# A two-layer hybrid decoder step: which products share the attention rounds, and where the gates are computed

## The chip, the cores and the metric

The kernel runs on one core of one Trainium2 chip. The metric is the device time of one launch in microseconds (us). A core has TensorE for matmuls (PE; its weight loads are PEld), VectorE (DVE), ScalarE (ACT), GpSimd (POOL) and SyncE (SP, which here only issues DMAs). Line numbers L... are those of the kernel before.

## The reference

Two groups of tokens go through two layers: a prompt of 256 positions and 8 samples of 8 positions each (together T = 320 columns), model width 1024. Each layer computes

```
xn = RMSNorm(x);  h = xn @ w_in                       # 1024 x 7344, split into the parts below
A: causal means over 2/4/8/16 positions minus the token, a 128 x 128 map per group, * silu(z_pool)
B: latent attention with 8 heads; the samples attend to 2048 cached positions each, * silu(z_mla)
C: a convolution over 4 positions on q, k, v; L2 norms; a chunked gated delta rule, 8 heads; * silu(z_dn)
gates = sigmoid(h_gate)                               # 3 branches x 1024
merged = gates[0] * (y_a @ w_br_pool) + gates[1] * (y_b @ w_br_mla) + gates[2] * (y_c @ w_br_dn)
x = x + merged @ w_out
```

After the second layer comes a last RMSNorm. Keys, conv rows, pooling rows and delta states are outputs too.

## The kernel before, in words

Activations stand transposed, features on the 128 partitions and the 320 tokens along the free dimension. A product in near-float32 precision is made of three: weights and activations are each split into a high and a low part in fp32r, and `mm3` (L214 to L226) issues high x high, high x low and low x high for each of the 8 (or 4) blocks of 128 rows. So 128 columns of `w_in` or `w_out` take 24 matmuls of 128 x 128 weights and 320 columns, and 128 columns of a branch matrix (512 rows) take 12. `load_w` (L178) fetches the raw weights through SP into one of four buffers; `split_w` (L186) writes the high part on ACT (L200) and the low part on DVE (L201), or on POOL where the running number of the split in the layer stands in the table entry 'lo'.

Each layer runs through these stages:

1. *Convolution.* `unit` (L535) projects 128 columns of q or k, scales them by `rn` on DVE (L500, L501), applies four taps (the first on ACT, three on DVE at L509), tanh on ACT, and a square on POOL (L542) for the L2 norm. POOL also copies the last rows for the state output (L503, L504). `value` does the same for v, `pooling` and `pool_gate` handle branch A, `zproj` (L434) the z of the other branches. These are *fillers*, taken from a list in the order of the table entry 'fo' by `fill(n)` (L705).
2. *Inversion.* The delta rule needs the inverse of a triangular matrix for each chunk; it is built by DVE steps (L760 to L774) and three levels of small products (L789 to L820), with fillers between them (entries 'f8', 'fy', 'fz').
3. *U and W, then delta.* The chunk products, and a loop over five chunks that carries the state, again with fillers ('ft', 'fu', 'fn'): late z's, queries and keys.
4. *Heads.* Attention of the prompt, head by head, with two gates between them.
5. *Rounds.* Eight rounds bb, one for each sample: scores against its 2048 gathered keys (144 matmuls, L1186), a maximum and an exponential, the turning of the weights by transposes (L1234), the product with the values (L1257), while DVE turns the next sample's keys (L1176).
6. *End.* Branch products for 8 blocks m and three branches n, sums in `accs`, then `w_out` and the norm of the next layer.

A gate (`gate_w`, `gate_mm`, `gate_out`, L451 to L468) is 24 matmuls, a product with `rn` on DVE (L464) and a tanh on ACT (L465). The 24 gates of a layer are independent of all else after xn, so they are put wherever PE might idle, in the order of the list `order`: all three branches for blocks 0 and 1, then 2 and 3, and so on. The table entries 'ga', 'gm', 'gb', 'gc', 'gs', 'gq' say how many go behind the decay products, behind each inversion level, and so on; `GL` says how many go into each round. A gate stays in one of 11 SBUF buffers (tag gt) or is *spilled*: written to DRAM through ACT's queue and read back through POOL's (L1353) when its branch product is due. `branch_out` (L1350) multiplies product and gate on DVE; branch 0 writes the sum `accs[m]`, the other two are added to it on POOL (L1361).

In the heads, the rounds and the start of the end stage the order on each engine is the program's (`manual_schedule`, L1369). Elsewhere a planner orders the instructions of each engine from estimated times; a DMA goes out in its queue's order. Each engine then works strictly in its order.

## Time and profile before

| | |
|---|---|
| median of 3 runs | 1044.32 us (1042.73 to 1047.79) |
| the profiled execution | 1044.8 us, of which 1042.8 us are the span from the first to the last instruction |
| PE, PEld, DVE, ACT, POOL busy | 987.6, 865.2, 712.1, 466.5, 332.2 us |
| mean granted clock of TensorE | 0.973 |
| HBM read, written | 144.17 MB, 13.68 MB |

Busy times overlap, since the engines work side by side. A granted clock of 1.00 is the higher of the two levels (2.4 GHz), 0.5 the lower (1.2 GHz); a mean between them tells how much of a stretch ran at either.

In layer 0 the convolution runs from about 26 to 103 us, the inversion to 169, U, W, delta and heads to 314, the rounds to 449, the end stage to 528. Layer 1 repeats this: convolution 528 to 613, inversion to 667, rounds from 816, end from 950.

### The profile page before, as it was taken

To read this page: it belongs to the slowest core of one execution; us is meant where nothing else is said; L and a number is where in the kernel's file an instruction comes from. 1 tells how busy PE (TensorE), PEld (TensorE's weight loads), DVE (VectorE), ACT (ScalarE), POOL (GpSimd) and SP (SyncE) were. 2 spreads that over 40 slices of the span, in tenths; PEclk is the share of its full clock that TensorE was granted. 3 is DMA by queue.
4 is the path that set the end of the run, shared out by engine and by line. 5 is a ranking of instruction groups with operands and counts; after the bars stand their busy time and mean duration, and the time that the engine had idled before them with its cause. 6 is when DMAs were issued, how large, how long until landed. Compare 5 with 4: busy or idle time off the path is not lost.

```text
span 1042.8 us, 24809 instructions
## 1 busy us (share of the span) xinstructions
PE 987.6 (95%) x10211; PEld 865.2 (83%) x10211; DVE 712.1 (68%) x1353; ACT 466.5 (45%) x838; POOL 332.2 (32%) x467
## 2 busy tenths in 40 slices
PE   8988899999999999999989979999999999998996
PEld 6877798997878888789978868999887787877996
DVE  3899974658656666677758988646774675754962
ACT  5554253555443333444546534336455333334453
POOL 3656312124250101035445542221334201100631
PEclk8999899999999999999999989999999999999999
DMA  9533324633656776268563333455256577633861
GB/s 235 158 82 101 96 74 111 184 96 91 203 171 202 242 233 225 78 196 233 144 194 94 86 98 82 109 144 140 71 145 232 163 227 259 189 135 126 237 171 51
DMA packets 202698, 159.22 MB, mean 153 GB/s; under 512 B 27704, under 2 KB 191826, under 8 KB 200010
## 3 DMA queue, kind: packets, MB, share of 16 engines
q1 hardware_dynamic: 176364, 98.47, 34.7%
q0 software_dynamic: 7424, 48.75, 13.2%
q10 hardware_dynamic: 18798, 10.44, 3.5%
q8 instruction: 80, 1.31, 0.5%
q14 instruction: 32, 0.26, 0.1%
HBM read 144.17 MB, written 13.68 MB: 151 GB/s over the span
## 4 chain that ended last, share of the span: by engine, by line
PE 73%; DVE 16%; ACT 5%; issue 3%; DMA 2%; POOL 1%; SPq 0%; DVEq 0%; ACTq 0%; POOLq 0%
PE sc L1186 6%; PE pv L1257 6%; PE pj L224 5%; PE gate L224 5%; PE pj L226 5%; PE pj L225 5%; PE gate L226 5%; PE gate L225 4%; DVE cy L509 4%; DVE wl L201 3%; PE br L226 3%; PE br L224 3%; PE br L225 3%; PE wo L224 2%; PE wo L225 2%
## 5 line engine op out<-in xcount | busy, mean ns | idle before, releaser
L201 DVE TENSOR_TENSOR wl<-wraw,wh 128x1024 fp32r<-128x1024 f32 (+2 forms) x169 | 195.9, 1167 | 83.0 <-ACT wh L200 82.0
L200 ACT ACTIVATE wh<-wraw 128x1024 fp32r<-128x1024 f32 (+1 forms) x180 | 166.5, 935 | 156.4 <-PE pj L225 75.8
L224 PE MATMUL pj<-xnH,wh 128*128 128x320 f32 (+1 forms) x528 | 172.7, 327 | 13.0 <-DVE V L501 7.6
L226 PE MATMUL pj<-xnH,wl 128*128 128x320 f32 (+1 forms) x528 | 170.2, 322 | 6.3 <-DVE wl L201 6.0
L225 PE MATMUL pj<-xnL,wh 128*128 128x320 f32 (+1 forms) x528 | 168.6, 319 | 0.0
L224 PE MATMUL gate<-xnH,wh 128*128 128x320 f32 x384 | 125.4, 326 | 1.7 <-DVE V L501 1.5
L226 PE MATMUL gate<-xnH,wl 128*128 128x320 f32 x384 | 121.2, 316 | 2.2 <-DVE wl L201 1.8
L225 PE MATMUL gate<-xnL,wh 128*128 128x320 f32 x384 | 120.1, 313 | 0.0
L224 PEld LDWEIGHTS pj<-xnH,wh 128*128 128x128 f32 (+1 forms) x528 | 101.8, 193 | 19.0 <-ACT wh L200 7.7
L226 PEld LDWEIGHTS pj<-xnH,wl 128*128 128x128 f32 (+1 forms) x528 | 101.7, 193 | 10.6 <-DVE wl L201 7.9
L225 PEld LDWEIGHTS pj<-xnL,wh 128*128 128x128 f32 (+1 forms) x528 | 101.7, 193 | 4.9 <-issue 3.5
L224 PEld LDWEIGHTS gate<-xnH,wh 128*128 128x128 f32 x384 | 73.4, 191 | 9.3 <-issue 5.7
L1176 DVE STREAM_TRANSPOSE KT<-kv 128x1024 f32<-128x1024 f32 x64 | 78.6, 1228 | 0.5
L226 PEld LDWEIGHTS gate<-xnH,wl 128*128 128x128 f32 x384 | 73.3, 191 | 4.0 <-DVE wl L201 2.6
L225 PEld LDWEIGHTS gate<-xnL,wh 128*128 128x128 f32 x384 | 73.5, 191 | 1.1 <-issue 0.8
L224 PE MATMUL br<-yH,wh 128*128 128x320 f32 x192 | 61.1, 319 | 3.0 <-ACT wh L200 2.6
L226 PE MATMUL br<-yH,wl 128*128 128x320 f32 x192 | 60.4, 316 | 1.8 <-DVE wl L201 1.8
L225 PE MATMUL br<-yL,wh 128*128 128x320 f32 x192 | 60.2, 314 | 0.0
L1186 PE MATMUL sc<-KT,q 32*64 32x256 f32 x2048 | 59.3, 377 | 0.0
L1257 PE MATMUL pv<-kv,PT 128*64 128x256 f32 x512 | 58.8, 382 | 0.2
L509 DVE SCALAR_TENSOR_TENSOR cy<-V,prm,cy 128x344 f32<-128x344 f32 x72 | 56.4, 802 | 0.5
L1186 PEld LDWEIGHTS sc<-KT,q 32*64 32x64 f32 x2048 | 45.8, 131 | 12.0 <-issue 5.7
(410 smaller groups left out, 2045.1 us busy)
## 6 DMA issues: line engine op xcount, KB each, us to landing
wraw<-in_w_in SPq DMA_DIRECT2D x114, 512.0 KB
wraw<-in_w_out SPq DMA_DIRECT2D x16, 512.0 KB
q<-q4d SPq DMA_DIRECT2D x64, 72.0 KB
gate<-gt ACTq DMA_DIRECT2D x28, 160.0 KB
gt<-gate POOLq DMA_DIRECT2D x28, 160.0 KB, 3.5
wraw<-in_w_br_pool SPq DMA_DIRECT2D x16, 256.0 KB
wraw<-in_w_br_dn SPq DMA_DIRECT2D x16, 256.0 KB
wraw<-in_w_br_mla SPq DMA_DIRECT2D x16, 256.0 KB
```

What stands on the lines that cost most here:

```text
L200: act(h, raw, AF.Copy)
L201: (nc.gpsimd.tensor_tensor if spare or turn[0] in K["lo"] else tt)(lo, raw, h.bitcast(F32), sub)
L224: nc.tensor.matmul(out, wh[:, k, :], xh[:, first + k, :], start=k == 0, stop=False)
L225: nc.tensor.matmul(out, wh[:, k, :], xl[:, first + k, :], start=False, stop=False)
L226: nc.tensor.matmul(out, wl[:, k, :], xh[:, first + k, :], start=False, stop=k == nk - 1)
L509: stt(y, V[:, j : j + 344], wj(j), y, mult, add)
L1176: nc.vector.transpose(v[:, a], kv[:, a * 1024 : a * 1024 + 1024].rearrange("p (i k c) -> p i k c", i=4, k=8))
L1186: nc.tensor.matmul(sc[64 * hf : 64 * hf + 64, g, :256], q4[r, k, :], krT[r, keys_] if k == 8 else KT[r, k, keys_], start=k == 0, stop=k == 8,)
L1257: nc.tensor.matmul(pv[64 * hf : 64 * hf + 64, :256], PT[:, n * 128 + 64 * hf : n * 128 + 64 * hf + 64], kv[:, r : r + 256], start=n == 0, ...
```

## The change

- `order` holds the gates of branches 1 and 2 only, 16 of them. All are spilled to DRAM. They are all computed before the rounds: one behind the small columns and one behind the next unit ('g0'), three inside the list of fillers (entry -1 in 'fo'), one behind the decay products, one behind each of the first two inversion levels, one in the U/W part, three in the delta loop, two behind it, two in the heads.
- Each round computes the gate of branch 0 for m = bb, directly followed by that branch's product for the same m; gate times product goes to DRAM as `sums[m]` (through ACT's queue) and is read back as the start of `accs[m]` (through POOL's). The split of `zs[0..3]` that these products need moves from the last round to the end of the delta stage.
- The end stage has 16 branch products, those of branches 1 and 2, instead of 23, and in layer 1 no late gate any more.
- Squares (L542) and the state copies (two on POOL, now a strided one) move to ACT. 'lo' is empty: every low part of a weight split is made on DVE.

Table entries that differ (before, then after; where the layers differ, layer 0 / layer 1):

| entry | what it counts | before | after |
|---|---|---|---|
| kk | fillers around the decay products | 1, 1, 2, 3 | 2, 1, 3, 4 |
| g0 | gates behind the small columns, behind the next unit | none | 1, 1 |
| ga | gates behind the decay products | 3 | 1 |
| fy | fillers between a level's two products | 2, 1, 1 / 2, 1, 2 | 2, 2, 2 |
| fz | fillers behind a level | 1, 1, 1 / 1, 0, 1 | 1, 1, 2 |
| gm | gates behind a level | 0, 2, 0 / 0, 0, 0 | 1, 1, 0 |
| gb | gates behind the inversion | 0 / 1 | 0 |
| gc | gates in the U/W part | 0, 0, 0 | 0, 1, 0 |
| gs | gates in the delta loop | 0, 0, 2, 1, 0 | 0, 1, 1, 1, 0 |
| gq | gates behind the delta stage | 0 | 2 |
| lo | splits with the low part on POOL | 1, 2, 4, 5, 8, 13 / 1, 2, 4, 5, 15 | none |
| GL | gates in rounds 0 to 7 | 2, 2, 2, 2, 2, 2, 1, 1 | 1 each, with the branch product |
| fo | fillers before the late ones | 20, and one z_dn | 19, three z_dn, three gates |

In 'fo' of layer 0 the order becomes 0, -1, 1, 2, -1, 3, 4, -1, 5, 6, 20, 18, 19, 7, 21, 8, 12, 9, 13, 10, 14, 11, 15, 22, 16, 17 (0 to 3 units, 4 to 7 values, 8 to 11 pooling, 12 to 15 its z, 16 and 17 without products, 18 and 19 the latent keys, 20 to 22 z_dn); before it was 0 to 9, 12, 13, 10, 14, 11, 18, 15, 16, 17, 19.

The rest of the diff, cut to its core:

```diff
@@ -32,16 +32,16 @@
 THB = 2
-NG = 11
+NG = 6
...
-GL, SPILL = (2, 2, 2, 2, 2, 2, 1, 1), 14
+SPILL = 16
...
@@ -442,14 +442,15 @@
         branches = ((0, "w_br_pool", 0), (2, "w_br_dn", 8), (1, "w_br_mla", 4))
-        order = [(n, 2 * mp + i) for mp in range(4) for n in range(3) for i in range(2)]
+        order = [(n, 2 * mp + i) for mp in range(4) for n in (1, 2) for i in range(2)]
...
-        def gate_w(spare=False):
-            n, m = order.pop(0)
+        sums = [tc.dram_tile([128, T], F32, name=f"sum{l}_{m}") for m in range(8)]
+        def gate_w(spare=False, nm=None):
+            n, m = nm or order.pop(0)
...
@@ -458,20 +459,33 @@
-        def gate_out(nm, b, spill=False):
-            t = per.tile([128, T], F32, tag="gs" if spill else "gt", name="gt", bufs=2 if spill else NG)
+        def gate_out(nm, b):
+            t = per.tile([128, T], F32, tag="gs", name="gt", bufs=3)
...
             act(t, t, AF.Tanh, scale=0.5)
-            if spill:
+            if nm[0]:
...
                 nc.scalar.dma_start(spilled[nm], t)
-            else:
-                early[nm] = t
-        def gate(tag, spare=False, spill=False):
-            nm, w = gate_w(spare)
-            gate_out(nm, gate_mm(tag, w), spill)
+            return t
+        def gate(tag):
+            nm, w = gate_w()
+            gate_out(nm, gate_mm(tag, w))
+        yb = {}
+        def split_hi(pool, y0):
+            yb[y0] = (pool.tile([128, 4, T], F32R, name=f"yH{y0}"), pool.tile([128, 4, T], F32R, name=f"yL{y0}"))
+            for i in range(4):
+                act(yb[y0][0][:, i, :], zs[y0 + i], AF.Copy)
+        def split_lo(y0):
+            for i in range(4):
+                tt(yb[y0][1][:, i, :], zs[y0 + i], yb[y0][0][:, i, :].bitcast(F32), sub)
+        def split_y(pool, y0):
+            split_hi(pool, y0)
+            split_lo(y0)
...
@@ -500,8 +514,9 @@
             nc.gpsimd.tensor_copy(Vs[:, :, :3], stT[:, ct, :].rearrange("p (b j) -> p b j", j=3))
-            nc.gpsimd.tensor_copy(cnew[:, ct, 0:3], V[:, 256:259])
-            nc.gpsimd.tensor_copy(cnew[:, ct, 3:27].rearrange("p (b j) -> p b j", j=3), Vs[:, :, 8:])
+            last3 = bass.AP(V.tensor, V[:, 256:].offset, [V.ap[0], [11, 9], [1, 3]])
+            act(cnew[:, ct, 0:27].rearrange("p (b j) -> p b j", j=3), last3, AF.Copy)
...
@@ -539,7 +554,7 @@
             sq = pt.tile([128, T], F32, tag="sq", name="sq", bufs=2)
-            nc.gpsimd.tensor_tensor(sq, o, o, mult)
+            act(sq, o, AF.Square)
...
@@ -610,7 +625,11 @@
+        for _ in range(K["g0"][0]):
+            gate("pj")
         unit(0, 2)
+        for _ in range(K["g0"][1]):
+            gate("pj")
...
@@ -692,12 +711,10 @@
         fillers += [lambda i=i: tt(hkv[:, i, :], proj(C_KV + 128 * i), rn, mult) for i in range(2)]
-        fillers = [fillers[i] for i in K["fo"]]
...
         gated += [lambda i=i: zproj(4 + i, C_ZMLA + 128 * i) for i in range(4)]
-        for z, at in zip(gated, K["zp"]):
-            if at >= 0:
-                fillers.insert(at, z)
+        fillers = [gated[i - 20] if i >= 20 else fillers[i] if i >= 0 else lambda: gate(chunk.get("tag", "pj")) for i in K["fo"]]
...
@@ -1008,7 +1025,7 @@
         late = [keys, keys_out, queries, transposed_wuk, latent_queries, *gated, *uqs]
-        fillers += [late[i] for i in K["to"] if not 5 <= i < 13 or K["zp"][i - 5] < 0]
+        fillers += [late[i] for i in K["to"] if not 5 <= i < 13 or i + 15 not in K["fo"]]
...
@@ -1112,8 +1129,10 @@
         fill(99)
+        split_y(p2, 0)
...
             gate("pj")
+        assert len(order) == 2, order
...
@@ -1323,21 +1342,6 @@
-        yb = {}
-        def split_hi(pool, y0):
-            yb[y0] = (pool.tile([128, 4, T], F32R, name=f"yH{y0}"), pool.tile([128, 4, T], F32R, name=f"yL{y0}"))
-            for i in range(4):
-                act(yb[y0][0][:, i, :], zs[y0 + i], AF.Copy)
-        def split_lo(y0):
-            for i in range(4):
-                tt(yb[y0][1][:, i, :], zs[y0 + i], yb[y0][0][:, i, :].bitcast(F32), sub)
-        def split_y(pool, y0):
-            split_hi(pool, y0)
-            split_lo(y0)
...
@@ -1348,21 +1352,20 @@
         def branch_out(n, m, b):
-            if (n, m) in spilled:
-                t = per.tile([128, T], F32, tag="gt", name="gt", bufs=NG)
-                nc.gpsimd.dma_start(t, spilled[n, m])
-            else:
-                t = early[n, m]
-            if n == 0:
+            t = per.tile([128, T], F32, tag="gt", name="gt", bufs=NG)
+            nc.gpsimd.dma_start(t, spilled[n, m])
+            if m not in accs:
                 accs[m] = p3a.tile([128, T], F32, tag="acc", name="acc", bufs=4)
-                stt(accs[m], t, 1.0, b[:, :T], add, mult)
-            else:
-                stt(t, t, 1.0, b[:, :T], add, mult)
-                nc.gpsimd.tensor_tensor(accs[m], accs[m], t, add)
+                nc.gpsimd.dma_start(accs[m], sums[m])
+            stt(t, t, 1.0, b[:, :T], add, mult)
+            nc.gpsimd.tensor_tensor(accs[m], accs[m], t, add)
+        def first_sum(m, t, b):
+            stt(t, t, 1.0, b[:, :T], add, mult)
+            nc.scalar.dma_start(sums[m], t)
         def branch(n, m, tag):
-            if (n, m) not in spilled and (n, m) not in early:
-                gate("pj")
...
@@ -1415,12 +1418,12 @@
                 if h == 3:
-                    gate_out(nm, b, True)
+                    gate_out(nm, b)
...
                 if h == 8:
-                    gate_out(nm, b, True)
+                    gate_out(nm, b)
                     pair[0] = paired[0] = 1
-                    gs = [gate_w() for _ in range(GL[0])]
+                    gs = gate_w(nm=(0, 0)), branch_w(0, 0)
...
@@ -1437,7 +1440,6 @@
                     p3a = p3e.enter_context(tc.tile_pool(name=f"p3a_{l}", bufs=1, reuse_waits="tile"))
-                    split_hi(p3a, 0)
...
@@ -1446,49 +1448,38 @@
                     flip(bb + 1, keys, 1)
-                else:
-                    split_lo(0)
-                    w00 = branch_w(0, 0)
-                g = [(gs[0][0], gate_mm("A", gs[0][1]))]
+                (nm, w), w0 = gs
+                g = gate_mm("A", w)
...
                     combined(bb - 1, ob)
-                gate_out(*g[0], bb < 6)
+                t = gate_out(nm, g)
...
                     flip(bb + 1, keys, 2)
-                two = len(gs) > 1
-                if two:
-                    b = gate_mm("A", gs[1][1], ks=(0, 4))
...
                 PTn = turned_own(bb)
-                if two:
-                    gate_mm("A", gs[1][1], b, (4, 8))
-                    gate_out(gs[1][0], b, bb < 6)
-                if not more:
-                    b00 = branch_mm(0, w00, "A")
+                b = branch_mm(0, w0, "A")
...
                 if not more:
-                    w01 = branch_w(0, 1)
+                    w10 = branch_w(1, 0)
                     split_y(p3a, 8)
+                    w11 = branch_w(1, 1)
                 o = attend(bb, PT, PTn, mx)
+                first_sum(bb, t, b)
...
                     flip(bb + 1, keys, 3)
-                    gs = [gate_w() for _ in range(GL[bb + 1])]
+                    gs = gate_w(nm=(0, bb + 1)), branch_w(0, bb + 1)
...
             wuv = load_wuv(pb.tile([128, 1024], F32, tag="S", name="wuv", bufs=2))
-            branch_out(0, 0, b00)
-            b01 = branch_mm(0, w01, "A")
-            if order:
-                gate("A")
-            w10 = branch_w(1, 0)
+            b10 = branch_mm(1, w10, "A")
             combined(NB - 1, combine(o))
-            b10 = branch_mm(1, w10, "A")
-            branch_out(0, 1, b01)
-            w11 = branch_w(1, 1)
+            b11 = branch_mm(1, w11, "A")
+            branch_out(1, 0, b10)
+            w12 = branch_w(1, 2)
...
@@ -1497,7 +1488,8 @@
                 stt(zs[4 + p][:, TP:], b[:, p * 64 : p * 64 + 64], 0.5, zs[4 + p][:, TP:], mult, mult)
-            b11 = branch_mm(1, w11, "A")
+            branch_out(1, 1, b11)
+            b12 = branch_mm(1, w12, "A")
...
@@ -1508,24 +1500,23 @@
             wcfg.update(pool=p3, n=2)
+            w13 = branch_w(1, 3)
+            split_y(p3, 4)
             w20 = branch_w(2, 0)
-            split_y(p3, 4)
-            branch_out(1, 0, b10)
-            w02 = branch_w(0, 2)
-            branch_out(1, 1, b11)
-            b02 = branch_mm(0, w02, "A")
+            b13 = branch_mm(1, w13, "A")
+            branch_out(1, 2, b12)
...
             b20 = branch_mm(2, w20, "A")
-            branch_out(0, 2, b02)
+            branch_out(1, 3, b13)
...
             branch_out(2, 1, b21)
-        early_br = {(0, 0), (0, 1), (1, 0), (1, 1), (0, 2), (2, 0), (2, 1)}
+        early_br = {(1, 0), (1, 1), (1, 2), (1, 3), (2, 0), (2, 1)}
...
         for mp in range(4):
-            for n in range(3):
+            for n in (1, 2):
...
```

## Rows read from the trace of the kernel before

**Rows 1.** The page: span, and busy time of each engine.
```profile
span 1042.8 us, 24809 instructions
...
PE 987.6 (95%) x10211; PEld 865.2 (83%) x10211; DVE 712.1 (68%) x1353; ACT 466.5 (45%) x838; POOL 332.2 (32%) x467
```

**Rows 2.** Windows: length; busy (count) of PE, PEld, DVE, ACT, POOL; PEclk, DMA, GB/s.
```profile
26.00:103.00 77.00, 68.28 (x471) 60.72 (x470) 69.50 (x122) 41.50 (x64) 47.28 (x73) 0.96 0.41 112
103.00:169.00 66.00, 61.92 (x683) 56.50 (x683) 52.25 (x114) 26.12 (x40) 18.91 (x26) 0.95 0.37 100
...
314.00:417.00 103.00, 103.00 (x1434) 84.70 (x1425) 68.39 (x127) 36.12 (x67) 13.22 (x23) 1.00 0.70 228
...
457.00:493.00 36.00, 35.74 (x233) 35.74 (x234) 30.52 (x47) 14.40 (x24) 20.87 (x25) 0.95 0.80 229
...
545.00:613.00 68.00, 63.08 (x438) 56.71 (x437) 60.08 (x108) 38.46 (x58) 38.01 (x62) 0.94 0.37 96
613.00:667.00 54.00, 47.44 (x589) 43.45 (x590) 45.38 (x103) 19.95 (x31) 14.79 (x22) 0.91 0.30 80
```

**Rows 3.** The chain of waits by line, 26 to 103 and 103 to 169 us.
```profile
by line: DVE cy L509 23.9%; issue 7.6%; DVE wl L201 4.9%; PE gate L226 3.5%; DVE co L520 3.3%; ACT ct L511 3.2%; PE pj L221 3.1%; DVE kk L516 2.5%; PE gate L224 2.5%; DVE V L500 2.4%; PE gate L225 2.4%; PE G L737 2.3%; DVE a L751 2.2%; DVE 
...
by line: PE pj L224 13.8%; PE pj L226 12.8%; DVE wl L201 12.3%; PE pj L225 11.6%; issue 4.7%; PE Z L813 3.5%; PE Y L797 3.3%; DVE qq L552 2.6%; PE mix L651 2.4%; PE gate L226 2.2%; DVE cy L509 2.1%; ACT l L550 2.1%; ACT l L549 2.1%; DVE TS 
```

**Rows 4.** Timeline of attention round 3 on PE, then ACT.
```profile
370.02 0.31 PE L225 MATMUL gate<-xnL,wh 128*128 128x320 f32 x1
...
373.25 0.31 PE L226 MATMUL gate<-xnH,wl 128*128 128x320 f32 x1
...
373.75 0.39 PE L224 MATMUL gate<-xnH,wh 128*128 128x320 f32 x1
...
375.60 1.04 PE L1234 MATMUL PT<-cst,S 128*128 128x128 f32 x8
...
373.19 1.15 ACT L1216 ACTIVATE S<-S,mx 128x1024 f32<-128x1024 f32 x1 [5.02 <-DVE mx L1215]
```

**Rows 5.** The chain of waits: start, us, what; scores of rounds 5 to 7.
```profile
400.12 4.07 PE sc L1186 x144
...
417.30 4.15 PE sc L1186 x144
...
431.64 4.16 PE sc L1186 x144
```

**Rows 6.** Groups of instructions by form: busy us, mean ns of one.
```profile
L1361 POOL TENSOR_TENSOR acc<-acc,gt 128x320 f32<-128x320 f32 x32 | 37.4, 1174 | 33.1 <-DVE gt L1360 27.1 <-DMA wraw<-in_w_br_pool 5.9
...
L201 POOL TENSOR_TENSOR wl<-wraw,wh 128x1024 fp32r<-128x1024 f32 x11 | 26.6, 2420 | 13.9 <-ACT wh L200 13.8
...
L464 DVE TENSOR_TENSOR gt<-gate,rn 128x320 f32<-128x320 f32 x48 | 23.2, 483 | 35.3 <-PE gate L226 35.2
...
L1353 POOL DMA_DIRECT2D gt<-gate x28 | 15.4, 551 | 34.6 <-DVE acc L1358 31.7 <-POOL acc L1361 2.4 <-issue 0.5
...
L504 POOL COPY cnew<-V 128x24 f32<-128x24 f32 x24 | 9.8, 409 | 0.0
...
L542 POOL TENSOR_TENSOR sq<-qq 128x320 f32<-128x320 f32 x8 | 8.0, 994 | 10.5 <-DVE qq L520 9.8 <-PE pj L226 0.6
```

**Rows 7.** DMA queues: packets, MB, share of 16 engines.
```profile
q1 hardware_dynamic: 176364, 98.47, 34.7%
q0 software_dynamic: 7424, 48.75, 13.2%
```

**Rows 8.** Timeline on DVE, then POOL, in the convolution stretch of layer 0.
```profile
40.22 1.21 DVE L201 TENSOR_TENSOR wl<-wraw,wh 128x1024 fp32r<-128x1024 f32 x1
...
49.96 2.41 DVE L509 SCALAR_TENSOR_TENSOR cy<-V,prm,cy 128x344 f32<-128x344 f32 x1
...
67.65 0.57 DVE L509 SCALAR_TENSOR_TENSOR cy<-V,prm,cy 128x344 f32<-128x344 f32 x1
...
49.60 2.40 POOL L201 TENSOR_TENSOR wl<-wraw,wh 128x1024 fp32r<-128x1024 f32 x1
```

2 lines of the change are left out of this document (1 added, 1 removed).

## The prediction

> **What bounds the kernel now.** I read the page first. PE is busy 95% of a span of 1042.8 us [rows 1], so little seems left to win, but the end of a matmul is modelled, and a matmul that runs at the lower clock counts as busy too. The Trainium skill ("Perfetto Trace Analysis", Identifying the Most-Contended Engine) calls matmul busy time a poor measure of headroom and wants the weight loads instead; here these are busy 83%, so by that page more is open than the 5%. I did not build on that sentence; I cut the span into stages instead and looked at each.
>
> The windows [rows 2] are to be read as busy time against length. In the attention rounds with two gates (314 to 417 us) PE is busy 103.00 of 103 us. In the product loop behind them (457 to 493) it is busy 35.74 of 36. These two are full: work taken out of them shortens them. In the convolution stretch of layer 0 (26 to 103) PE has 68.28 of 77 us, in the inversion behind it (103 to 169) 61.92 of 66; in layer 1 the same two have 63.08 of 68 (545 to 613) and 47.44 of 54 (613 to 667). The granted clock is 0.91 to 0.96 there, so part of the busy time runs at the lower of the two levels; a shortfall of 0.09 over 54 us is 4.9 us of full-speed work. Idle plus clock: 8.7 + 3.1 and 4.1 + 3.3 us in layer 0, 4.9 + 4.1 and 6.6 + 4.9 in layer 1, together 40 us. Nothing else in the kernel is as empty.
>
> Who holds PE up there is in the chain of waits [rows 3]: from 26 to 103 the largest share is the DVE taps of the convolution (L509, 23.9%), and DVE is busy 69.50 of 77 us [rows 2]; from 103 to 169 the products of the projections lead (13.8, 12.8 and 11.6%) and the weight split on DVE follows with 12.3%. So the first stretch is DVE's, the second mostly PE's.
>
> **What is moved.** Neither the products nor their number change. A *unit* is a projection or a gate: 24 matmuls. Back to back their starts lie (373.25 - 370.02) / 22 = 0.147 us apart [rows 4], so a unit is 3.52 us of PE and a branch product of 12 is 1.76. Counting calls from the tables: the convolution stretch gets 3 more units in either layer (6 gates for 3); the inversion gets 3 in layer 0 and 4 in layer 1 (two delta-branch z's, and one or two gates more); the U/W part and the delta stage swap units one for one. That is 13 units, 45.8 us of PE. Out go, behind the rounds, 7 branch products in each layer and one late gate in layer 1: 12.3 + 15.8 = 28.1 us. A round had 48 gate matmuls in rounds 0 to 5 and 24 in round 6; it gets 24 + 12.
>
> **Rounds.** Round 5 takes 417.30 - 400.12 = 17.18 us, round 6, with one gate, 431.64 - 417.30 = 14.34 [rows 5]. The 12 matmuls that vanish are those ahead of the turning of the weights, 373.75 to 375.60 = 1.85 us [rows 4]. They covered a wait: the exponential ends at 373.19 + 1.15 = 374.34, and PE would now be ready at about 373.9, so 0.5 us comes back as idle. New round: 17.18 - 1.85 + 0.5 = 15.8. Six rounds save 1.35 each, round 6 grows by 1.5 (its gap behind the turning is filled by the new product); round 7 has what it had. That gives -6.6 per layer, **-13.2**; bounds -17 (the whole 60 matmuls of either layer) and -8 (0.5 us more waiting per round).
>
> **Product loop and the end.** The window 457 to 493 is full, so the 28.1 us come off whole if its feeds keep up. POOL: three issues (two loads, every second time the sum) of 0.55 and two additions of 1.17 per pair of products [rows 6] make 4.0 us against 3.52 of PE; but ten loads (six gate buffers, four sums) can be issued during the rounds, which leaves 14 x 0.55 + 16 x 1.17 = 26.4 against 28.2 of PE. Transfers: 16 weights of 256 KB on queue 1 and 24 loads of 160 KB and xT (1.3 MB) on queue 0. The rows give 98.47 MB in 34.7% of the span, 272 GB/s, and 48.75 in 13.2%, 354 GB/s [rows 7]; 4.2 MB and 5.2 MB are then 15.4 + 14.8 = 30 us, beside 28 us of products and what is fetched ahead of them. Both are close. I charge 1 us a layer, **+2** (bounds 0 and 8), and the end gives **-28.1**.
>
> **Convolution stretch.** It belongs to DVE, so DVE's sum counts. Three gates, each a split and a product with rn, bring 3 x (1.2 + 0.48) = 5.0 us in each layer [rows 6, 8]. Emptying 'lo' brings the six (layer 1: five) POOL splits to DVE at 1.2: 7.2 and 6.0. Against this stands what POOL no longer does: these splits (2.42 each) and eight squares a layer (about 1 us each) [rows 6], the small state copies besides. While POOL ran a split from 49.60 to 52.00, a tap beside it took 2.41 us instead of 0.57 [rows 8], 1.84 lost. Six such are 11 us, the squares at most 8 more; the other end is nothing. I take 9 and, for five splits, 7.5, nearest to the splits' own row, since it is the only one that shows a loss directly. The rule in the Trainium skill ("SBUF — State Buffer", Who interferes with whom) is that a DVE operation with two SBUF inputs is locked out for the whole of a GpSimd operation that reads SBUF; the trace agrees (2.41 us). The Trainium skill ("Perfetto Trace Analysis", Optimizing Scalar/DVE Operations) warns that shifting work between these two engines might not help; by that the relief would be no more than the splits cost, 7.2 and 6.0, and the sum 3 us worse. Net +3.2 and **+3.5**. PE's 10.6 us of new work fits into its 11.8 (9.0) us of idle and clock plus this growth.
>
> **Inversion.** New PE work 10.6 and 14.1 us; room 7.4 and 11.5. It cannot all be used, as the level products still wait for DVE between the units: I take 5 and 8, two thirds, which leaves **+5.6** and **+6.1**; bounds are all of the room and none.
>
> Costed at nothing: squares and the strided state copy on ACT, at most 8 x 1 + 12 x 0.4 us a layer by what they took on POOL [rows 6], and its extra DRAM issues; ACT is busy 41.50 of 77 us there [rows 2]. If that cover is gone, the copy stands ahead of the first tap in ACT's order, and the DVE chain is late by its length, 5 us a layer. The extra y split before the heads lies beside the two gates put there. On SP the w_in loads only come earlier; the DMA share there is 0.30 to 0.41 [rows 2]. Waits added: a gate's tile returns after its DRAM write, with three buffers; DVE's next gate product would queue behind it. The branch loads in POOL's order wait for six buffers instead of eleven; behind them stand the additions.
>
> **Sum.** 3.2 + 3.5 + 5.6 + 6.1 = 18.4 of growth, - 13.2 - 28.1 + 2 = -20.9. The profiled execution took 1044.8 us (span 1042.8 and 2.0 around it), so 1023.9; the median of the runs shown is 0.5 lower: 1023.4, say **1023**.
>
> **Rivals.**
> - *More is absorbed.* With the new units PE never falls to the lower clock, and the inversion takes its work in whole: growth 8 instead of 18.4, 1013 us. For it: PE's room, 40 us, is nearly the 45.8 added. Against: the waits are on DVE, and DVE gets no emptier. Chance 0.22.
> - *DVE is the bound throughout.* No relief from POOL (growth 12.2 + 11.0) and a third of the room used in the inversion (8 + 10): growth 41, 1046 us, no change. For it: 69.50 of 77. Against: row pair 49.60/49.96 [rows 8]. Chance 0.12. The Trainium skill ("Perfetto Trace Analysis", Identifying the Most-Contended Engine) has the engine of highest occupancy unloaded first; from 26 to 103 us that is DVE, and the change loads it.
> - *Slower: the convolution starves.* PE takes its work in order; a gate put between two convolutions delays by 3.52 us the product that DVE wants next, and DVE's chain lengthens instead of running beside it. Then nothing is absorbed and the units cost their full 45.8 us, a tenth of it more at the lower clock: growth 50, 1055 us. It decides from a growth of 45 on. Against: DVE has a backlog nearly all through. Chance 0.08.
> - *The gates do not stay where they are put*, since outside the hand-written part a planner orders the engines; they drift into full stretches, and little changes: about 1040. Chance 0.03.
>
> **Numbers.** The forecast has 0.55. A change under 0.5%, 5.2 us, cannot be told from none. Faster: 0.55 + 0.22 = 0.77; the same: 0.12 + 0.03; slower 0.08. The range runs from 1008 (all absorbed, rounds at their bound) to 1043 (the middle of the DVE case); outside lie the slower case, half of the DVE case and a little below, 0.18.
>
> **What would show it.** Right: rounds 0 to 6 of 15.8 us; 28 us less between the last scores and the next layer; the convolution and inversion stretches 3 and 6 us longer, at a granted clock near 1.00; no POOL splits, and taps of 0.57 with few of 2.4. Wrong: PE gaps put down to DVE as large as before in these stretches; POOL or the loads of gt and acc as what releases PE in the loop; rounds still at 17.

## The result: slower by 2.7%, and the profile after

The changed kernel takes 1072.33 us (median of 4 runs, 1067.52 to 1076.39) against 1043.53 us (1042.03 to 1047.79, 4 runs) for the kernel before, measured beside it: a ratio of 1.0267, 95% interval 1.0212 to 1.0323. The forecast was 1023 us with a range from 1008 to 1043, so the sign and the size are wrong. The profiled execution took 1067.52 us, of which 1065.8 are the span. Line numbers are now those of the changed kernel (the addition is L1361 in both, the gate's product with the branch is L1360, loads L1356 and L1359, queries' and keys' squares L557).

The page, the answer to [rows 1]:

```profile
span 1065.8 us, 24832 instructions
...
PE 984.4 (92%) x10211; PEld 858.9 (81%) x10211; DVE 692.1 (65%) x1364; ACT 474.8 (45%) x878; POOL 279.2 (26%) x412
```

PE has the same 10211 matmuls and is busy 3 us less, in a span 23 us longer. Nothing was added to its work; it waits more. POOL lost 53 us of work, DVE 20. No engine became the bound as a whole, so the loss has to be found by stage. The table cuts every span at the same instructions: the first transpose of the convolution's state, the first sum R of the inversion, the first product of the delta loop (op), the first key product of the heads (kn), the first scores of rounds 0 and 7 (sc), the last matmul of the output projection (wo). Layer 0 / layer 1, in us:

| kernel | convolution | inversion, U, W | delta | heads | seven rounds | end |
|---|---|---|---|---|---|---|
| before | 85.0 / 80.5 | 89.5 / 81.5 | 88.6 / 88.2 | 32.4 / 32.5 | 117.8 / 117.8 | 90.6 / 98.9 |
| after | 84.1 / 78.8 | 100.0 / 96.6 | 92.3 / 99.1 | 34.0 / 32.5 | 114.2 / 114.0 | 88.0 / 95.3 |
| after - before, both layers | -2.6 | +25.6 | +14.6 | +1.6 | -7.4 | -6.2 |
| forecast | +6.7 | +11.7 | 0 | 0 | -13.2 | -26.1 |

The differences sum to 25.6 us; what lies ahead of layer 0's convolution, between the layers and behind the last stage is some 2.5 shorter, and 23.0 is the growth of the span. Against the forecast the end misses 19.9 us, delta 14.6, the inversion 13.9 and the rounds 5.8; the convolution did 9.3 better. Each is taken up below.

Windows of the changed kernel, columns as in [rows 2]: convolution and inversion of layer 0, inversion and delta of layer 1, seven rounds, 56 us of the end of layer 0.

```profile
17.60:101.70 84.10, 80.32 (x579) 74.17 (x579) 68.34 (x130) 52.49 (x93) 25.47 (x41) 0.98 0.56 158
101.70:179.60 77.90, 73.42 (x853) 68.52 (x852) 61.34 (x134) 31.57 (x47) 16.07 (x25) 0.98 0.46 124
618.10:692.30 74.20, 70.33 (x826) 66.30 (x826) 60.63 (x132) 31.69 (x47) 15.43 (x23) 1.00 0.45 122
714.70:813.80 99.10, 90.14 (x838) 79.00 (x835) 59.09 (x119) 45.64 (x80) 24.51 (x26) 0.93 0.43 119
328.00:442.20 114.20, 109.68 (x1596) 86.91 (x1595) 75.36 (x148) 36.00 (x71) 13.52 (x25) 1.00 0.60 197
450.00:506.00 56.00, 46.45 (x328) 42.12 (x327) 31.25 (x60) 21.08 (x40) 26.37 (x40) 0.97 0.71 213
```

The convolution is now nearly full (80.32 of 84.10, at 0.98). The end, whose product loop was full before (35.74 of 36 in [rows 2]), has 9.5 us of PE idle in its 56. The delta stage of layer 1, which was not to change, has 9.0 idle, at a clock of 0.93. In the rounds 4.5 us are missing.

The timeline of POOL at the end of layer 0 shows the first of these (columns: start, us, engine, line, what; in brackets the idle time before it and what ended it):

```profile
450.84 0.60 POOL L1356 DMA_DIRECT2D gt<-gate  x1 [0.28 <-DVE olat L1292]
451.44 0.56 POOL L1359 DMA_DIRECT2D acc<-sum  x1
460.75 1.24 POOL L1361 TENSOR_TENSOR acc<-acc,gt 128x320 f32<-128x320 f32 x1 [8.75 <-DVE gt L1360]
461.95 0.56 POOL L1356 DMA_DIRECT2D gt<-gate  x1
462.51 0.55 POOL L1359 DMA_DIRECT2D acc<-sum  x1
...
466.12 0.95 POOL L1361 TENSOR_TENSOR acc<-acc,gt 128x320 f32<-128x320 f32 x1 [2.53 <-DMA acc<-sum]
467.01 0.56 POOL L1356 DMA_DIRECT2D gt<-gate  x1
467.57 0.54 POOL L1359 DMA_DIRECT2D acc<-sum  x1
472.66 1.25 POOL L1361 TENSOR_TENSOR acc<-acc,gt 128x320 f32<-128x320 f32 x1 [4.54 <-DVE gt L1360]
```

One load of a gate and one of a sum go out, then POOL stands at the addition that needs both the loads and the product on DVE; the next two loads are issued only when that addition is done. DVE's products with the gate wait for these loads:

```profile
465.25 0.49 DVE L1360 SCALAR_TENSOR_TENSOR gt<-gt,br 128x320 f32<-128x320 f32 x1 [1.71 <-DMA gt<-gate]
472.09 0.49 DVE L1360 SCALAR_TENSOR_TENSOR gt<-gt,br 128x320 f32<-128x320 f32 x1 [2.26 <-DMA gt<-gate]
```

So a product waits for a trip to DRAM that began after the addition before it had ended. Six gate buffers are free and are of no use, since the load that would fill them stands behind an addition in an engine that works strictly in its order. The waits of PE in the same stretch (440 to 506 us; us in total, times, longest) show how it reaches PE: a product needs a PSUM bank, and the banks are freed by DVE's product with the gate, which waits for the load.

```profile
PE br L224 <- DVE gt L1360: 7.4, 4, 2.5
PE br L226 <- DVE wl L201: 2.1, 2, 1.3
```

### The profile page after: what moved, and what is told of

It reads as the page before. It is cut to its first block, busy times and chain, and to the rows that moved or that the text cites. A ratio compares the mean times of both kernels' runs of the same rounds, so it can differ in the third digit from the quotient of the medians.

```text
span 1065.8 us, 24832 instructions
## 1 busy us (share of the span) xinstructions
PE 984.4 (92%) x10211; PEld 858.9 (81%) x10211; DVE 692.1 (65%) x1364; ACT 474.8 (45%) x878; POOL 279.2 (26%) x412
## 5 line engine op out<-in xcount | busy, mean ns | idle before, releaser
L201 DVE TENSOR_TENSOR wl<-wraw,wh 128x1024 fp32r<-128x1024 f32 (+1 forms) x180 | 195.6, 1099 | 116.1 <-ACT wh L200 115.8
L224 PE MATMUL gate<-xnH,wh 128*128 128x320 f32 x384 | 122.2, 318 | 0.8 <-DVE qn L982 0.6
L224 PE MATMUL br<-yH,wh 128*128 128x320 f32 x192 | 63.8, 332 | 15.0 <-DVE gt L1360 14.9
L1235 ACT ACTIVATE S<-S,mx 128x1024 f32<-128x1024 f32 x16 | 18.4, 1149 | 84.5 <-DVE mx L1234 72.3
```

Of the source, the lines that this page charges most:

```text
L201: (nc.gpsimd.tensor_tensor if spare or turn[0] in K["lo"] else tt)(lo, raw, h.bitcast(F32), sub)
L224: nc.tensor.matmul(out, wh[:, k, :], xh[:, first + k, :], start=k == 0, stop=False)
L1235: act(S, S, AF.Exp, bias=mx[:, 4:5], accum_out=mx[:, 5:6])
```

## The experiments

The theory after the result had four parts: (1) at the end the loads are late because of POOL's order, not because DRAM is slow; (2) the delta stage lost because the z products moved out of it had covered its chain of dependent steps, although as many units stand there as before; (3) the inversion is paced by its products and absorbs little; (4) the rounds keep a wait for ACT. The rival for all four was that DVE, which took over POOL's splits, is late everywhere. The stage lengths of the runs, both layers added:

| kernel | median us | convolution | inversion, U, W | delta | rounds | end |
|---|---|---|---|---|---|---|
| before, beside these | 1044.6 to 1047.6 | 165.5 | 171.0 | 176.8 | 235.6 | 189.5 |
| after | 1072.3 | 162.9 | 196.6 | 191.4 | 228.2 | 183.3 |
| e1 loads early | 1051.1 | 165.2 | 197.1 | 192.0 | 228.4 | 157.7 |
| e2 z products back | 1065.1 | 164.8 | 197.6 | 183.0 | 228.3 | 182.6 |
| e3 work back on POOL | 1078.9 | 165.1 | 200.8 | 193.3 | 229.1 | 184.7 |
| e4 = e1 + e2 | 1042.1 | 165.3 | 198.8 | 183.7 | 228.0 | 159.6 |
| e5 before, POOL relieved | 1043.7 | 156.7 | 175.1 | 180.8 | 235.9 | 188.0 |
| e6 = e4 + split product | 1031.8 | 163.0 | 200.4 | 183.4 | 218.2 | 159.6 |
| e7 = e4, gates out of inversion | 1047.0 | 162.0 | 184.0 | 202.7 | 228.7 | 159.8 |
| e8 = e4, xT earlier | 1042.4 | 163.0 | 198.9 | 184.3 | 228.9 | 161.7 |
| e9 = e6 + queries on SP | 1028.0 | 164.0 | 198.7 | 179.0 | 218.4 | 158.6 |
| e10 = e6, less residual | 1031.2 | 166.2 | 200.2 | 184.2 | 218.2 | 160.6 |
| e11 = e9, all loads ahead | 1030.8 | 162.3 | 198.7 | 179.9 | 218.6 | 161.9 |

The convolution's code is the same from e4 on, but for e5, and its sum still varies from 162.0 to 166.2; a stage's length is good to some 4 us over both layers. The runs come from four chips (e1 to e4, e5 to e8, e9 and e10, e11), each beside the kernel before; across chips the ratios to it are safer to compare than the totals.

### e1: the loads issued ahead of the additions

```diff
-        def branch_out(n, m, b):
-            t = per.tile([128, T], F32, tag="gt", name="gt", bufs=NG)
-            nc.gpsimd.dma_start(t, spilled[n, m])
+        def branch_load(n, m):
+            early[n, m] = t = per.tile([128, T], F32, tag="gt", name="gt", bufs=NG)
+            nc.gpsimd.dma_start(t, spilled[n, m])
...
                     p3a = p3e.enter_context(tc.tile_pool(name=f"p3a_{l}", bufs=1, reuse_waits="tile"))
+                    for nm in ((1, 0), (1, 1), (1, 2), (1, 3), (2, 0), (2, 1)):
+                        branch_load(*nm)
```

> The changed kernel with one edit: the six gate loads and four sum loads that the hand-ordered end of a layer needs are issued together at the start of the last round, ahead of the additions, where the changed kernel has each pair of loads behind the addition of the product before it in POOL's order. If POOL's order is what stretches the end, the time from the first scores of round 7 to the first product with w_out falls from 56.2 and 56.9 us to about 50 in both layers, PE's waits for gt there (14.9 us) nearly vanish, and the time falls by 10 to 14 us, to about 1057. The rival is that the transfers themselves are the bound (weights, gates and sums together close to what the queues carry): then the stretch stays at 55 or more with a DMA share above 0.9, and the time falls by less than 3 us.

Measured: 1051.11 us (10 runs), 1.005 times the kernel before (1.0026 to 1.0075). Against the changed kernel that is 21 us less, more than the 10 to 14 expected, and the end falls from 88.0 and 95.3 to 76.9 and 80.8. The stretch from the first scores of round 7 to the first product with `w_out` takes 46.5 and 46.3 us (62.2 and 68.3 before the change), the output projection 30.3 and 34.5 (28.4 and 30.6). The same six gates and four sums cross the same queue; only their place in POOL's order differs. All that is left of waits on PE from 455 to 500 us in this kernel is:

```profile
PE wo L224 <- ACT mgH L209: 0.8, 2, 0.4
PE br L226 <- DVE wl L201: 0.6, 1, 0.6
```

The wait for the gate's product is gone, and with a DMA share of 0.68 from 443 to 489 us the rival, transfers as the bound, falls. The end is now 31.8 us shorter than before the change, where 26.1 were forecast, so none of the forecast's gain from the products is missing any more; why it is more is not shown.

### e2: the z products back in the delta stage

Two gates take the place of two z products among the inversion's fillers, the other gates' places go back to those of before; the number of units in the delta stage does not change by more than 0.3.

```diff
-'fo': [0, -1, 1, 2, -1, 3, 4, -1, 5, 6, 20, 18, 19, 7, 21, 8, 12, 9, 13, 10, 14, 11, 15, 22, 16, 17]
-'gs': [0, 1, 1, 1, 0], 'gq': 2
+'fo': [0, -1, 1, 2, -1, 3, 4, -1, 5, 6, -1, 18, 19, 7, -1, 8, 12, 9, 13, 10, 14, 11, 15, 23, 16, 17]
+'gs': [0, 0, 2, 1, 0], 'gq': 0
```

> The changed kernel with the z projections of the delta branch put back where they were (three of them in the delta stage, one in the U/W part) and gates in their places in the inversion, so that the number of units in each stage differs by one at most; the delta stage is again as before the change. If the z projections were the cover for the chains of keys and queries (their norms run on ACT and POOL while PE waits), the stretch from the first chunk product of the delta loop to its end loses its PE gaps again: about 3 us in layer 0, about 10 in layer 1, the time falls by 10 to 15 us. The rival is that units are only PE time, wherever they stand: then the time moves by less than 3 us either way.

Measured: 1065.05 us (4 runs), 1.0184 (1.0138 to 1.0229), 7.3 us below the changed kernel and short of the 10 to 15 expected. The delta stage of layer 1 falls from 99.1 to 90.8, that of layer 0 stays (92.3, 92.2). The waits of PE in layer 1, first of the changed kernel (714 to 814 us):

```profile
PE ws L1073 <- ACT rs L410: 2.1, 1, 2.1
PE uq L224 <- ACT cqH L206: 2.0, 1, 2.0
PE ckt L951 <- DVE hkv L942: 1.6, 2, 1.1
```

then of e2 (714 to 806 us):

```profile
PE pj L224 <- ACT wh L200: 2.9, 1, 2.9
...
PE ckt L951 <- DVE hkv L942: 0.4, 1, 0.4
```

The waits for the latent queries' norm (rs, cqH) and for the keys (hkv) are the chain that the z products had covered. A gate put behind that chain ('gq') cannot cover it. With these waits goes most of the low clock: the stage's granted clock is 0.93 in the changed kernel and 0.98 in e2. About 1 us of the 8.3 is a third of a unit that slipped from this stage into the inversion.

Layer 0 has the same waits in the changed kernel (200 to 300 us), at a granted clock of 1.00:

```profile
PE ckt L951 <- DVE hkv L942: 1.5, 2, 1.0
PE us L1080 <- ACT rs L410: 1.3, 1, 1.3
PE uq L224 <- ACT cqH L206: 1.0, 1, 1.0
```

In e2 they are gone there too, but for 0.4 us, and another stands in their place:

```profile
PE oT L1128 <- DVE so L1021: 2.6, 1, 2.6
PE ckt L951 <- DVE hkv L942: 0.4, 1, 0.4
```

So part (2) holds in both layers; in layer 0 its gain is eaten by a wait that the changed kernel does not have. e9 takes it up.

### e3: the work back on POOL

```diff
-            act(sq, o, AF.Square)
+            nc.gpsimd.tensor_tensor(sq, o, o, mult)
...
-            act(cnew[:, ct, 0:27].rearrange("p (b j) -> p b j", j=3), last3, AF.Copy)
+            nc.gpsimd.tensor_copy(cnew[:, ct, 0:3], V[:, 256:259])
+            nc.gpsimd.tensor_copy(cnew[:, ct, 3:27].rearrange("p (b j) -> p b j", j=3), Vs[:, :, 8:])
...
-'lo': []
+'lo': [1, 2, 4, 5, 8, 13]
```

> The changed kernel with the squares and state copies on POOL again and the eleven weight splits whose low part POOL made. If taking these off POOL frees DVE (taps no longer locked out), putting them back costs 4 to 6 us in each convolution stretch (its end is late by that in both layers), and the time rises by 8 to 12 us. The rival, that shifting work between these two engines changes nothing, or that DVE is the loser by the extra splits: the time stays within 3 us or falls by up to 5.

Measured: 1078.91 us (4 runs), 1.0301 (1.0254 to 1.0347), 6.6 us above the changed kernel, where 8 to 12 were expected. The two intervals overlap (1.0212 to 1.0323 for the changed kernel), so the totals do not show that the relief was a gain; nor do the convolutions, 4.3 us longer in layer 0 and 2.1 shorter in layer 1. What is shown is that putting the work back wins back none of the 29 us that were lost: the rival, that the loss is DVE's new work, falls.

### e4: both repairs

> The changed kernel with both edits, early loads and the z projections back. If the two losses lie in different stages and have the causes named, they add: 20 to 28 us less than the changed kernel, 1040 to 1048 us. If one of them only moves the wait on (the end then waits for weights, the delta stage for ACT), the sum is under 15 us and the time stays above 1053.

Its edit is that of e1 and e2 together. Measured: 1042.12 us (10 runs), 0.9961 (0.9944 to 0.9977): the two repairs add up (21.2 and 7.3 alone, 30.2 together), and the change is worth 0.4% after all.

### e5: the relief of POOL alone, in the kernel before

The edit is that of e3 turned round, in the kernel before.

> The kernel before with one part of the change alone: the squares of queries and keys and the copies of the convolution's state go from POOL to ACT, and no residual of a weight is subtracted on POOL. No unit is added. Theory (POOL held the convolution back in the kernel before, and its relief paid for the three units that the changed kernel fits in): the convolution stretch falls by 3 to 5 us in each layer from 85.0 and 80.5 us, the total by 5 to 10 us below the kernel before. Rival (the changed kernel's units only filled gaps that were there anyway, and POOL held nothing back): the stretch and the total stay within 2 us.

Measured: 1043.68 us (10 runs), 0.9995 (0.9973 to 1.0017). Both were half right: the convolution falls by 4.7 and 4.1 us, as the theory had it, but the total does not. The inversion with U and W grows by 7.4 in layer 1 (0.8 of a unit, 2.8 us, slipped into it) and falls by 3.3 in layer 0, and delta grows by 2.3 and 1.7. How the relief works is shown by the taps of the convolution, grouped by form from 18 to 103 us (busy us, mean ns of one); first the kernel before:

```profile
L509 DVE SCALAR_TENSOR_TENSOR cy<-V,prm,cy 128x344 f32<-128x344 f32 x33 | 27.0, 837 | 0.3
```

then e5:

```profile
L509 DVE SCALAR_TENSOR_TENSOR cy<-V,prm,cy 128x344 f32<-128x344 f32 x33 | 21.4, 662 | 2.3 <-ACT cy L507 2.1
```

The same 33 taps take 175 ns less each, 5.6 us, without POOL's splits and squares beside them.

### e6: the branch product of a round cut in two

```diff
+                b = branch_mm(0, w0, "A", ks=(0, 2))
                 PT = turned_p(S)
                 PTn = turned_own(bb)
-                b = branch_mm(0, w0, "A")
+                branch_mm(0, w0, "A", b, (2, 4))
```

> The version with both repairs (early loads, z products back; 1042.1 us), and in each round the branch's product is cut in two: six matmuls ahead of the transposes of the softened scores, six behind them. Theory (a round still has some 0.65 us in which TensorE waits for ACT's last piece of the softened scores, and nothing else is short): rounds fall from 16.1 to about 15.6 us, 4 us a layer, total about 1034 us. Rival (the second half is then too short to cover ACT's copies of the transposed weights, so the wait moves behind them to the value products): rounds stay within 0.2 us of 16.1, total 1040 to 1043 us.

Measured: 1031.84 us (6 runs), 0.987 (0.9841 to 0.9899). A middle round falls from 16.1 to 15.4 us, seven of them from 114.0 to 109.2 and 109.0. The chain of waits (start, us, what) has the scores of rounds 2 to 4 of e6 at:

```profile
361.90 4.07 PE sc L1205 x144
377.32 4.07 PE sc L1205 x144
392.73 4.07 PE sc L1205 x144
```

and the waits for ACT's softened scores fall in layer 0 from this in the changed kernel (325 to 442 us):

```profile
PE PT L1253 <- ACT S L1235: 4.5, 7, 1.4
```

to this in e6 (325 to 436 us):

```profile
PE PT L1253 <- ACT S L1235: 0.5, 1, 0.5
```

Six matmuls behind the transposes still cover ACT's copies: no wait took this one's place, and the rival falls.

### e7: three gates out of the inversion

```diff
-'gm': [1, 1, 0], 'gc': [0, 1, 0], 'gq': 0
+'gm': [0, 0, 0], 'gc': [0, 0, 0], 'gq': 3
```

> The version with both repairs, and the three gates that were put among the inversion's own steps are computed by themselves behind the delta stage, in both layers: same work, another place. Theory (the inversion stage is paced by its products and had next to no room left, so that a unit costs about as much there as by itself): the stretch from the sums R to the end of U and W falls by 8 to 10 us a layer, the stretch behind it grows by as much, and the total stays at 1042 within 3 us. Rival (two thirds of each unit's time are hidden there, as forecast): the stretch falls by only 3 to 4 us a layer and the total rises by 12 to 14 us.

Measured: 1047.00 us (12 runs), 1.0013 (0.9989 to 1.0036), 4.9 us above e4. The inversion with U and W gives back 14.8 us in both layers together, delta grows by 19.0. Six gates are 6 x 3.52 = 21.1 us of PE, so some seven tenths of a gate's time are exposed in the inversion: more than the forecast had, which left 11.7 of its 24.7 us exposed, just under half (not a third, as the expectation puts it). The total lies between theory and rival, nearer to the theory. The layers differ: 10.3 us come back in layer 1, 4.5 in layer 0.

### e8 and e10: is the end held by the DMA engines?

With the pooling branch gone from the end, its 10 us from 985 to 995 in e4 show a DMA share of 1.00 at 289 GB/s. e8 moves the 1280 KB of xT to an earlier place, e10 leaves out seven eighths of them.

```diff
             wcfg.update(pool=p3, n=2)
+            xT = p3.tile([128, 8, T], F32, name="xT")
+            nc.gpsimd.dma_start(xT, xs[l])
...
-        xT = p3.tile([128, 8, T], F32, name="xT")
-        nc.gpsimd.dma_start(xT, xs[l])
```

> The version with both repairs, and the load of the layer's input for the residual (1280 KB) is issued where its buffer first exists, some 15 us earlier. Theory (with the pooling branch gone from the end, the 16 DMA engines are full there: share 1.00 and 1.02 of their time from 985 to 1005 us, which holds up the output weights): the load moves into the stretch with share 0.67, and the output projection of the second layer falls by 2 to 4 us from 37.4, total 1038 to 1041 us. Rival (the output weights are late because their buffers come free late, or the earlier load pushes back the branches' weights and gates instead): no gain, 1041 to 1045 us.

```diff
-        nc.gpsimd.dma_start(xT, xs[l])
+        nc.gpsimd.dma_start(xT[:, 0, :], xs[l][:, 0, :])
...
-                tt(xT[:, m, :], xT[:, m, :], b[:, :T], add)
+                tt(xT[:, m, :], xT[:, 0, :], b[:, :T], add)
```

> The version with the two repairs and the split branch product, with seven eighths of the load of the layer's input left out at the end (the residual of every group of columns is taken from the first group; the sum computed is another, its instructions are the same). It takes 1120 KB from the end of each layer, where the DMA engines are busy all the time for some 10 us (share 1.06 at 309 GB/s from 978 to 988 us). Theory (the end is now held by the 16 DMA engines, moving a load within it only moves the delay, and only less traffic helps): the end of the second layer, from the last scores to the end of the output projection (82.0 us), falls by 3 to 4 us, the first layer's by 1 to 3, total 1026 to 1028 us. Rival (the output weights are late because their buffers come free late): both ends within 1 us, total 1031 to 1033 us.

Measured: e8 1042.37 us (12 runs), 0.9973 (0.9955 to 0.9991), the same as e4; its output projection in layer 1 fell by 1.3 us, and the products ahead of it grew by 2.0. e10 1031.19 us (4 runs), 0.9859 (0.9828 to 0.9889), the same as e6; its ends are 76.0 and 84.6 against 77.6 and 82.0. The theory falls. The rival's late buffers are not shown either; from 945 us on PE's two longest waits in e10 are for the split of the merged sums, not for a weight:

```profile
PE wo L224 <- ACT mgH L209: 2.2, 3, 1.0
PE wo L225 <- DVE mgL L210: 0.9, 2, 0.6
```

With 1120 KB less the windows of e10 still read, from 970 to 990 us:

```profile
970.00:980.00 10.00, 10.00 (x70) 10.00 (x69) 10.00 (x17) 4.65 (x9) 6.89 (x11) 1.00 0.86 251
980.00:990.00 10.00, 8.80 (x55) 7.69 (x53) 7.47 (x7) 4.15 (x5) 5.72 (x7) 1.00 1.07 309
```

In these 20 us seven weights of the output projection, 512 KB each, are issued and take 70% of the engines' time. A full share by itself did not mean here that PE was waiting for transfers.

### e9: the latent queries' transfers on another queue

```diff
-                nc.scalar.dma_start(q4d[:, :, k, :], qlat[32 * (k % 4) : 32 * (k % 4) + 32, k // 4])
+                nc.sync.dma_start(q4d[:, :, k, :], qlat[32 * (k % 4) : 32 * (k % 4) + 32, k // 4])
```

The wait that e2 brought into layer 0 (PE oT) is still there in e6, where ACT's timeline shows its cause:

```profile
279.80 5.19 ACTq L1013 DMA_DIRECT2D q4d<-qlat  x8
285.10 0.47 ACT L439 ACTIVATE th<-zs 128x320 f32<-128x320 f32 x1 [9.92 <-issue]
285.58 1.28 ACT L1120 ACT_TABLE_LOAD   x1
...
288.50 0.31 ACT L1121 ACTIVATE r<-r,epsc 128x20 f32<-128x20 f32 x1
```

DVE has the sums for the norm of the delta outputs at 281.49 (its reduction began at 280.02 and took 1.47), but ACT is issuing eight transfers, and the result comes at 288.81.

In the kernel before the planner had put the same norm ahead of the eight transfers. In the changed kernel they stood ahead of it too (273.25 us), but DVE's sums came only behind them, so that ACT waited 1.39 us for the sums, and PE was busy from 260 to 294 us without a gap: the two gates behind the delta stage ('gq') covered the norm (one of them runs just ahead of the transposes oT of its result, one between their two parts). e2 moved them away; e7, with three gates in that place, has no wait at oT either. In e6 PE waits 2.64 us until DVE has multiplied with the norm (288.85 to 290.34; the waits name DVE's next instruction, so), and the windows of e6 show what follows (columns as in [rows 2]):

```profile
288.00:290.60 2.60, 0.07 (x2) 0.07 (x4) 1.75 (x3) 2.54 (x4) 0.00 (x0) 0.80 0.00 0
290.60:293.00 2.40, 2.33 (x40) 2.14 (x40) 2.17 (x6) 1.33 (x5) 0.00 (x0) 0.50 0.00 0
293.00:296.00 3.00, 2.54 (x41) 2.42 (x42) 1.91 (x6) 0.85 (x1) 0.00 (x0) 0.50 0.00 0
296.00:299.00 3.00, 3.00 (x8) 2.37 (x9) 1.59 (x2) 0.76 (x2) 1.83 (x2) 0.50 0.09 13
```

The clock reads 0.50, the lower level, for the 8.4 us behind the wait.

> The version with the two repairs and the split branch product (1031.8 us), and the eight transfers of the latent queries to DRAM are issued on SP instead of ACT. In the first layer's delta stage of that version they stand on ACT's queue ahead of the normalisation of the delta outputs and hold it for 5.19 us; TensorE then waits 2.64 us for that result, and its granted clock reads 0.80, 0.50, 0.50 and 0.50 in the slices behind it. Theory (the planner's order on ACT, not the number of units, is what lengthens the first layer's delta stage): the wait and the low clock go, the stage falls from 92.5 to 86 to 88 us, the total to 1025 to 1028 us. Rival (on SP the transfers hold back the weight loads behind them, and TensorE waits for a weight instead): the stage stays at 91 to 94 us, the total at 1031 to 1035 us.

Measured: 1027.98 us (6 runs), 0.984 (0.9814 to 0.9867). The delta stage of layer 0 falls from 92.5 to 88.2 us, that of layer 1 stays (90.9, 90.8). ACT now has the norm early:

```profile
281.45 0.31 ACT L1120 ACTIVATE r<-r,epsc 128x20 f32<-128x20 f32 x1 [5.06 <-DVE r L1119]
281.78 1.28 ACT L1121 ACT_TABLE_LOAD   x1
283.07 0.31 ACT L1121 ACTIVATE r<-r,epsc 128x20 f32<-128x20 f32 x1
```

and the clock in e9 behind the same place is whole:

```profile
288.00:290.00 2.00, 1.23 (x42) 1.09 (x39) 1.96 (x5) 1.78 (x4) 0.00 (x0) 1.00 0.15 53
290.00:292.00 2.00, 1.93 (x44) 1.72 (x41) 1.52 (x4) 0.00 (x0) 0.00 (x0) 1.00 0.00 0
```

The totals of e6 and e9 have intervals that overlap; it is the stage, 92.4 to 92.5 us in layer 0 of e4, e6 and e10 and 88.2 and 88.0 in e9 and e11, that shows the gain. This is the version with the lowest median: 1.6% below the kernel before.

### e11: all loads of the end ahead

```diff
+        gpool[0] = p3, 10
+        rest = [(n, m) for mp in range(4) for n in (1, 2) for m in (2 * mp, 2 * mp + 1) if (n, m) not in early_br]
+        for nm_ in rest:
+            branch_load(*nm_)
         for mp in range(4):
```

> The version with the two repairs, the split product and the latent queries on SP (1028.0 us), with all ten remaining gates and the remaining sums of a layer's end loaded ahead of the remaining additions on POOL's queue (ten gate buffers from the space of the last stage, eight sum buffers in place of four). In that version POOL still stood 0.66 to 1.26 us at three loads of a sum whose buffer was not free, and the last two gates of the second layer were issued at 974.16 and 975.55 us and used at 983.79 us only; TensorE waited 1.06 us for what follows from them. Theory (the rest of the end's loss is again the order on POOL: loads behind additions): from the last scores to the end of the output projection 81.5 us of the second layer fall by 3 to 5 us, 77.1 of the first by 0 to 2, total 1022 to 1026 us. Rival (the last gates are late because DVE's queue has the subtractions of the output weights ahead of them, or the loads in one go hold back the weights on the DMA engines): both ends within 1 us or longer, total 1027 to 1032 us.

Measured: 1030.84 us (6 runs), 0.9844 (0.9811 to 0.9878): no gain over e9. Both parts are seen in layer 1: the output projection falls from 35.2 to 32.8 us, and the products ahead of it grow from 46.3 to 50.5. ACT's waits from 955 to 972 us in e11 say why:

```profile
ACT wh L200 <- DMA wraw<-in_w_br_mla: 8.0, 2, 7.8
```

Ten gates, a sum and xT go out in little over 8 us, and ACT stands 7.8 us for a branch weight that was issued among them; PE then waits 2.7 us. Loads ahead of the additions helped, all of them at once did not. What holds the output projection of layer 1 at 35.2 us in e9 (30.6 before) is not settled.

## Why the prediction was wrong, step by step

- **The end, -26.1 forecast, -6.2 measured: the largest miss.** The step that failed is "ten loads (six gate buffers, four sums) can be issued during the rounds". Two were, in either layer. The sentence was about buffers, and buffers were there; the order on POOL's queue, written out by hand in this stretch, puts each load behind the addition of the product before. The prediction even named what would show it wrong, loads of gt and acc as what releases PE, and the profile has that one step removed: PE is released by DVE's product, and DVE's product by the load of gt. Put right (e1), the end gave 31.8 us.
- **Delta, 0 forecast, +14.6 measured (3.7 in layer 0, 10.9 in layer 1).** The step is "swap units one for one". The count was right (13.0 units before, 12.5 after, by the matmuls recorded), the conclusion was not: a unit is worth what it covers. The z products stood beside a chain of dependent steps; the gates that replaced them behind it could not cover it, in either layer. e2 got back 8.3 us in layer 1. In layer 0 it only exchanged the loss: the chain's waits went, but the gates that had covered the norm of the delta outputs went too, and eight transfers ahead of that norm on ACT then cost 4.3 us (e9).
- **Inversion, +11.7 forecast, with U and W +25.6 measured.** Two errors. One is the count: 3 and 4 units were expected and none in U and W, but 3.4 and 6.0 came by the matmuls recorded (half a unit of each in U and W), 33.3 us in place of 24.7; one unit of layer 1's surplus had been meant for the convolution. The other is "two thirds" of the idle and of the low clock: growth of 10.5 and 15.1 us against 12.0 and 21.3 us of work leaves 1.5 and 6.2 us hidden, not 5 and 8. In layer 1 PE's idle in the inversion fell from 6.2 to 3.9 us and the clock rose from 0.91 to 1.00, as forecast; how the hidden time divides between these two is not shown. e7 puts the exposed part of a gate at seven tenths.
- **Rounds, -13.2 forecast, -7.4 measured.** The mechanism was right, the size off. The waits for ACT in layer 0 are 1.4 us in round 0 and 0.5 in each other one, the forecast's 0.5. But round 0 saved only 0.18 us (17.54 to 17.36) where the forecast took 1.35 for it as for the rest, a middle round saved 1.07 (17.18 to 16.11), 0.28 less than forecast without more waiting, and round 6 grew by 1.8, not 1.5. That the wait is what can be won, e6 shows: split around it, the product gives 15.4 us, below the 15.8 of the forecast.
- **Convolution, +6.7 forecast, -2.6 measured.** The mechanism was right; the term that was mis-sized is the relief of POOL, net of DVE's new splits put at 3.3 us in both layers (9 + 7.5 less 7.2 and 6.0) and measured at 8.8 (e5). In layer 0 three units fitted into PE's idle time and low clock (76.28 of 85.00 us busy before at 0.93, 80.32 of 84.10 after at 0.98); in layer 1 only 1.9 of the three came. The Trainium skill ("Perfetto Trace Analysis", Optimizing Scalar/DVE Operations) has it that moving work between DVE and POOL might not help: for the whole kernel before the measurement agrees, since e5 gained nothing, while the stage did gain. Only the splits move between these two engines, though; squares and copies went to ACT, and no run parts them.
- **The slower rival** had a chance of 0.08 and another mechanism, a convolution that starves, which did not happen. 1072 us lay outside of every case. The steps on the end and on delta share one fault: buffers and units were counted, and no step asked what stands ahead of an instruction in its engine's order, or beside it.

## What to carry to other kernels

When a result is moved to DRAM and read back, look at what stands ahead of the read on the queue that issues it: a load behind an instruction that waits for the previous load's user makes every pass a full trip; here six free buffers did not help. Idle time in a stage is not all room: here seven tenths of an added gate were exposed in one that had some. A unit that is swapped for another must stand beside the same chain. Where a planner orders the queues, read its order anew after each change, the DMA issues on a compute engine's queue above all.

## What was not expected of the hardware

- A wait of 2.64 us on PE cost more than itself. In the 8.4 us behind it the granted clock read 0.50: the 40 small transposes took 2.40 us where the same 40 took 1.38 in the kernel before, where PE had waited 0.77 us at most, and the 16 key products 5.77 against 3.98.
- Eight issues of transfers on ACT's queue took 5.19 us, 0.65 each, during which ACT ran nothing else.
- Taps of the convolution take 837 ns in the mean beside POOL's splits and squares, 662 without (e5).
- A DMA share near 1.07 at 309 GB/s did not mean that the stage was bound by transfers: 1120 KB less changed no time (e10 against e6).
